# Five-wide u/gate pairs, block sums by accumulating DMAs, and v's scalings behind a bank copy

## The chip, the core and the metric

The kernel runs on one core of one Trainium2 chip. The metric is the device time of one execution in microseconds (us). A core has five engines that take their instructions in order and wait for one another by semaphores: TensorE (PE, the matmuls, with its weight loads shown apart as PEld), VectorE (DVE), ScalarE (ACT), GpSimd (POOL) and SyncE (SP). SP issues the plain loads; POOL issues the DMAs that add into their destination. All transfers are carried by the core's 16 DMA engines.

## The reference

Two layers on 256 tokens of width 2048, all in fp32. Layer 0 is a gated MLP with a causal position mixing, layer 1 a stick-breaking attention. The change lies in layer 0:

```python
proj = rms_norm(x) @ w_in                       # 2048 x 12288: [u | v | gate], 4096 wide each
u, v = gelu(proj[u]), rms_norm(gelu(proj[v]))
mixed = einsum('gts,bnsgc->bntgc', tril(w_s), v in chunks of 128 tokens) + bias   # 16 groups of 256 columns
y = u * mixed * silu(proj[gate])
h = x + y @ w_out
```

The products with `w_in` for u and gate are 2048 x 8192 weights, 64 MB, against 256 tokens.

## The kernel before

**Precision.** An fp32 operand is held as a high part and a rest (hi and lo), both in the fast fp32 format of TensorE, and a product takes three matmuls: hi x hi, lo x hi, hi x lo (`terms`, L119 to L121). The token side is split once. Every weight tile is split as it comes, by `cut` (L108 to L116): ACT casts hi (L114), DVE subtracts to get lo (L115). A cut mostly covers two 128-row tiles, 128 x 1024 elements, and then feeds 12 matmuls in a plain product (two tiles, two blocks of 128 tokens, three terms). There are five hi and five lo buffers.

**Pairs.** The 16 x 512-column blocks of u and gate are worked in eight `Pair`s (L233), numbered from 0; a pair is one block of u (j = 1) and one of gate (j = 0). In a part of a pair's 16 row tiles (k) the four quadrants (upper or lower half of those rows, block 0 or 1) are multiplied by a scheme with seven products in place of eight. `ks` says how many tiles the upper and the lower half each have. The quadrants are called b11, b12 (upper rows, first and second block), b21, b22 (lower rows). The products run in the order p1, p5 (`head`), p6, p2, p7, p3, p4 (`body`), and each takes ks x 3 matmuls. Some of them need sums of quadrants, and these are made in place: b11 becomes a difference of b12 and b11 behind p1 (`minus`, L286), takes b22 in behind p5 (L314), and takes b21 in behind p6 (`minus` again); b12 takes in b22 by an accumulating DMA that reads b22's rows from memory again (`plus`, L294). The tiles of a quadrant are held in groups of two: with ks = 4 there are groups 0 and 1, with ks = 5 a fifth tile is group 2. The fifth of b11 gets b22 by such a DMA as well, since b22's fifth is loaded late.

The row tiles outside the two halves are the "rest", 16 - 2 x ks of them, and are multiplied plainly: `column(0)` behind the body, and `column(1)`, whose steps of two tiles are spread by `run` between the blocks of the next pair. In all a pair has 192 - 3 x ks matmuls.

**Banks.** The products are gathered in banks a, b, c, d, e of the result memory. ACT copies one bank into the next as the scheme wants it (L326 b from a, L331 c from b, L338 d from c, and L328 `es`, a copy of e), and DVE adds es to b and c.

**Mixing.** Behind p4 each pair calls `mixing` (L592): the position weights ws come by a POOL DMA (L597) issued behind the pair's last accumulating one, are masked on POOL (L602), and are split on ACT (wh, L604) and DVE (wl, L605), both held behind the copy to d. v, scaled to its norm, is split into vh (ACT, L610) and vl (DVE, L611). Six matmuls follow (L617 to L619), whose results ACT writes over v (L621). The finished columns go through an activation on ACT (L626) and products on DVE (L628, L533).

**Order.** Every engine's order is fixed when the kernel is built, by a scheduler that simulates the instructions with a model of their durations; `tc.issue_after(x)` holds an instruction behind x on its engine's list. SP's loads are issued in the order of the code. On POOL the accumulating DMAs, ws and the mask stand in one queue.

Of the kernel before, what the change touches and what calls it, by code (L numbers as in the profile page):

```python
# [20 lines left out]
KS_GU = (4, 4, 4, 5, 4, 5, 4, 4)  # L21
# [8 lines left out]
def trunk_kernel(ctx: ExitStack, tc: tile.TileContext, x, xt, gcols, wst, a_w_in, a_v_norm_g,  # L30
# [11 lines left out]
    nc = tc.nc  # L42
# [80 lines left out]
    class Left:  # L123
# [3 lines left out]
        def __init__(self, hi, lo):  # L127
            self.hi, self.lo, self.s, self.ks = hi, lo, [], 0
# [29 lines left out]
        def fifth(self, out, name):
# [8 lines left out]
            nc.vector.tensor_sub(sm[:, 0], a21, a22)  # L167
            nc.vector.tensor_sub(sm[:, 1], a11, sm[:, 0])
# [6 lines left out]
        def sums_of(self, y, ks, out, name):  # L175
# [10 lines left out]
            nc.vector.tensor_sub(s24, a11, s13)  # L186
# [3 lines left out]
            nc.vector.tensor_sub(s24, a12, s24)  # L190
# [42 lines left out]
    class Pair:  # L233
# [50 lines left out]
        def minus(self, into, b0, b1, order=None):  # L284
            for g in order or range(len(self.groups)):
                nc.vector.tensor_sub(into[g], b0[g], b1[g])  # L286

        def plus(self, into, i, j, g0=0):

            for g in self.early:  # L290
                if g < g0:
                    continue
                k, n = self.groups[g]
                adds.append(nc.gpsimd.dma_start(into[g], self.src(HALVES[i][k], n, j), accum_op=ALU.add))  # L294

        def head(self):
# [11 lines left out]
            self.minus(self.b11, self.b12, self.b11, self.early)  # L308
# [4 lines left out]
            for g in range(len(self.b22)):  # L313
                nc.vector.tensor_add(self.b11[g], self.b22[g], self.b11[g])  # L314
            self.plus(self.b11, 1, 1, len(self.b22))

        def body(self, between=lambda: None):
# [21 lines left out]
            self.minus(b11, b21, b11)  # L339
# [247 lines left out]
    with ExitStack() as lg:  # L587
# [4 lines left out]
        def mixing(b, pair):  # L592
# [15 lines left out]
            for t in range(NT):  # L608
                vs = v_of(t, b * CB, CB)
                nc.scalar.activation(vh[:, t], vs, AF.Identity, scale=rv[:, t:t + 1])  # L610
# [581 lines left out]
```

## Time and profile before

| | |
|---|---|
| time, median of 3 runs | 1144.05 us (1144.0 to 1144.16) |
| span of the profiled execution | 1142.0 us |
| time outside the span, against the median | 2.05 us |
| u/gate stage, from the first mixing's end of the windows view to the last | 150.5 to 488.5 us |
| loads by SP's queue (q1) | 227.57 MB, 58.9% of 16 DMA engines |
| by POOL's queue (q0) | 33.04 MB, 16.2% |

The profiled execution's own time is its span; what the device time has beyond it is not in the trace. The views used below are: the page (busy time of each engine; the chain of waits that ended last), the windows view (busy time of each engine in stretches of time, here from one mixing to the next), groups of instructions by line and shape (count, then total busy us, mean ns, and idle time ahead with what ended it), the timeline (start, duration, engine, line, operation; in brackets the idle time ahead and what ended it) and the DMA view (shares, queues, median us from issue to landing). "DVE gu_p_lo" is the lo half of a tile of one of the seven products, "gu_lo" that of a column's tile, "gu_b" a quadrant's tiles.

### The profile page before, as it was taken

How to read it: one execution, taken by the hardware profiler on the slowest of the kernel's cores; microseconds unless marked ns; L12 is line 12 of the kernel's file. 1: busy time of each engine (PE TensorE's matmuls, PEld its weight loads, DVE VectorE, ACT ScalarE, POOL GpSimd, SP SyncE). 2: the span in 40 equal slices, each digit the busy share in tenths (PEclk: the TensorE clock that was granted, in tenths of full speed). 3: DMA queues.
4: the chain of work that ended last, by engine and by line, in shares of the span. 5: the costliest groups of instructions: out<-in, count | busy, mean ns of one | idle time of the engine just before them, and what ended most of it. 6: DMA issues, size and time to landing. Idle time of an engine off the chain costs nothing.

```text
span 1142.0 us, 14838 instructions
## 1 busy us (share of the span) xinstructions
PE 1132.3 (99%) x5168; PEld 937.6 (82%) x5168; DVE 1010.9 (89%) x1111; ACT 828.5 (73%) x1102; POOL 99.8 (9%) x106
## 2 busy tenths in 40 slices
PE   9999999999999999999999999999999999999997
PEld 6788888888888888888888888888888888888886
DVE  7899889988998999978988678989889989897996
ACT  8776777777777778866657456788678887886564
POOL 0100110110110210100010001110100101100000
PEclk9999999999999999999999999999999999999999
DMA  9988788787797797685885868687687776837972
GB/s 335 317 290 270 214 252 270 194 266 241 173 274 249 191 261 240 177 296 142 267 259 166 276 203 282 153 280 211 181 283 200 211 230 174 272 88 241 325 225 92
DMA packets 135659, 264.72 MB, mean 232 GB/s; under 512 B 8992, under 2 KB 9504, under 8 KB 135456
## 3 DMA queue, kind: packets, MB, share of 16 engines
q1 hardware_dynamic: 117472, 227.57, 58.9%
q0 software_dynamic: 16304, 33.04, 16.2%
q10 hardware_dynamic: 1808, 3.17, 0.8%
q8 instruction: 40, 0.66, 0.2%
q14 instruction: 35, 0.29, 0.1%
HBM read 259.55 MB, written 4.19 MB: 231 GB/s over the span
## 4 chain that ended last, share of the span: by engine, by line
PE 93%; DMA 2%; DVE 2%; issue 1%; ACT 1%; SPq 0%; POOLq 0%; POOL 0%; ACTq 0%; DVEq 0%
PE gu_a L119 3%; PE gu_b L119 3%; PE gu_b L121 3%; PE gu_a L121 3%; PE gu_a L120 3%; PE gu_b L120 3%; PE op_acc L119 2%; PE op_acc L120 2%; PE op_acc L121 2%; PE gu_d L119 2%; PE gu_d L121 2%; PE gu_c L121 2%; PE gu_d L120 2%; PE gu_c L119 2%; PE gu_c L120 2%; PE qk_a L121 1%
## 5 line engine op out<-in xcount | busy, mean ns | idle before, releaser
L114 ACT CAST gu_p_hi<-gu_b 128x1024 fp32r<-128x1024 f32 (+1 forms) x126 | 122.9, 1004 | 38.4 <-DVE gu_b L314 16.1
L115 DVE TENSOR_TENSOR gu_p_lo<-gu_b,gu_p_hi 128x1024 fp32r<-128x1024 f32 (+1 forms) x126 | 142.8, 1165 | 1.9 <-ACT gu_p_hi L114 1.2
L115 DVE TENSOR_TENSOR qk_p_lo<-qk_b,qk_p_hi 128x1024 fp32r<-128x1024 f32 (+1 forms) x77 | 80.8, 1073 | 8.9 <-ACT qk_p_hi L114 8.4
L114 ACT CAST qk_p_hi<-qk_b 128x1024 fp32r<-128x1024 f32 (+1 forms) x77 | 70.5, 934 | 19.0 <-DMA qk_b<-in_b_w_in 4.0
L115 DVE TENSOR_TENSOR gu_lo<-gu_raw,gu_hi 128x1024 fp32r<-128x1024 f32 x60 | 72.1, 1218 | 12.5 <-ACT gu_hi L114 12.2
L114 ACT CAST gu_hi<-gu_raw 128x1024 fp32r<-128x1024 f32 x60 | 62.0, 1052 | 21.0 <-DMA gu_raw<-in_a_w_in 11.5
L115 DVE TENSOR_TENSOR v_lo<-v_raw,v_hi 128x1024 fp32r<-128x1024 f32 (+1 forms) x41 | 48.9, 1193 | 15.2 <-ACT v_hi L114 15.2
L114 ACT CAST v_hi<-v_raw 128x1024 fp32r<-128x1024 f32 (+1 forms) x41 | 41.7, 1028 | 27.9 <-DMA v_raw<-in_a_w_in 26.4
L115 DVE TENSOR_TENSOR v_p_lo<-v_b,v_p_hi 128x1024 fp32r<-128x1024 f32 x42 | 50.3, 1220 | 3.3 <-ACT v_p_hi L114 3.1
L114 ACT CAST v_p_hi<-v_b 128x1024 fp32r<-128x1024 f32 x42 | 43.0, 1049 | 9.8 <-PE v_c L121 4.9
L115 DVE TENSOR_TENSOR bg_p_lo<-bg_b,bg_p_hi 128x1024 fp32r<-128x1024 f32 (+1 forms) x42 | 42.5, 1041 | 4.8 <-ACT bg_p_hi L114 4.7
L114 ACT CAST o_p_hi<-o_b 128x1024 fp32r<-128x1024 f32 (+1 forms) x35 | 33.4, 965 | 18.1 <-PE op_acc L121 13.0
L115 DVE TENSOR_TENSOR bv_p_lo<-bv_b,bv_p_hi 128x1024 fp32r<-128x1024 f32 (+1 forms) x42 | 42.5, 1040 | 3.8 <-ACT bv_p_hi L114 3.6
L114 ACT CAST bv_p_hi<-bv_b 128x1024 fp32r<-128x1024 f32 (+1 forms) x42 | 37.4, 908 | 10.0 <-DMA bv_b<-in_b_w_in 3.0
L294 POOL DMA_DIRECT2D gu_b<-in_a_w_in x20 | 23.0, 1155 | 240.2 <-DVE gu_b L286 134.3
L114 ACT CAST bg_p_hi<-bg_b 128x1024 fp32r<-128x1024 f32 (+1 forms) x42 | 37.3, 907 | 8.0 <-PE bg_a L121 2.5
L115 DVE TENSOR_TENSOR o_p_lo<-o_b,o_p_hi 128x1024 fp32r<-128x1024 f32 (+1 forms) x35 | 38.3, 1113 | 5.4 <-ACT o_p_hi L114 5.4
L286 DVE TENSOR_TENSOR gu_b<-gu_b,gu_b 128x1024 f32<-128x1024 f32 (+1 forms) x36 | 41.4, 1169 | 0.1
L114 ACT CAST o_hi<-o_raw 128x1024 fp32r<-128x1024 f32 x22 | 23.0, 1052 | 24.9 <-DMA o_raw<-in_a_w_out 24.8
L115 DVE TENSOR_TENSOR o_lo<-o_raw,o_hi 128x1024 fp32r<-128x1024 f32 x22 | 26.7, 1221 | 15.2 <-ACT o_hi L114 15.0
L114 ACT CAST op_hi<-op_raw 128x1024 fp32r<-128x1024 f32 x24 | 25.1, 1053 | 19.3 <-PE op_acc L121 8.8
L120 PE MATMUL op_acc<-op_lo,yc 128*128 128x512 f32 x96 | 37.8, 393 | 0.0
(798 smaller groups left out, 3797.8 us busy)
## 6 DMA issues: line engine op xcount, KB each, us to landing
gu_b<-in_a_w_in SPq DMA_DIRECT2D x64, 512.0 KB, 4.8
gu_raw<-in_a_w_in SPq DMA_DIRECT2D x60, 512.0 KB, 5.4
v_raw<-in_a_w_in SPq DMA_DIRECT2D x39, 512.0 KB, 5.5
qk_b<-in_b_w_in SPq DMA_DIRECT2D x32, 512.0 KB, 5.3
qk_raw<-in_b_w_in SPq DMA_DIRECT2D x26, 512.0 KB, 5.5
v_b<-in_a_w_in SPq DMA_DIRECT2D x24, 512.0 KB, 5.4
op_raw<-in_a_w_out SPq DMA_DIRECT2D x24, 512.0 KB, 4.9
o_raw<-in_a_w_out SPq DMA_DIRECT2D x22, 512.0 KB, 4.7
```

The costliest lines, as they stand in the source:

```text
L114: nc.scalar.copy(hi[:, sl], raw[:, sl])
L115: low[0] = nc.vector.tensor_sub(lo[:, sl], raw[:, sl], f(hi[:, sl]))
L119: nc.tensor.matmul(acc, lh, hi, start=first, stop=False, skip_group_check=True)
L120: nc.tensor.matmul(acc, lh, lo, start=False, stop=False, skip_group_check=True)
L121: nc.tensor.matmul(acc, ll, hi, start=False, stop=last, skip_group_check=True)
L286: nc.vector.tensor_sub(into[g], b0[g], b1[g])
L294: adds.append(nc.gpsimd.dma_start(into[g], self.src(HALVES[i][k], n, j), accum_op=ALU.add))
```

## The change

There are three edits, all in layer 0's u/gate stage.

1. `KS_GU`, the ks of the eight pairs, goes from (4, 4, 4, 5, 4, 5, 4, 4) to (4, 5, 5, 5, 5, 5, 5, 4). Pairs 1, 2, 4 and 6 get a fifth tile in each half and one column step less in each column.
2. The sum b11 with b21 behind p6 is made by accumulating DMAs (`plus`) for the groups below `FAR_GU[b]`, and by DVE for the others. `FAR_GU` is (0, 2, 2, 1, 2, 1, 2, 1), so 11 groups of 1024 columns go to the POOL queue. [...]
3. vh's scalings are held behind the copy to d, as wh is, and vl follows them.

```diff
-KS_GU = (4, 4, 4, 5, 4, 5, 4, 4)
+KS_GU = (4, 5, 5, 5, 5, 5, 5, 4)
+FAR_GU = (0, 2, 2, 1, 2, 1, 2, 1)
...
-        def plus(self, into, i, j, g0=0):
+        def plus(self, into, i, j, g0=0, g1=9):
 
             for g in self.early:
-                if g < g0:
+                if not g0 <= g < g1:
                     continue
                 k, n = self.groups[g]
                 adds.append(nc.gpsimd.dma_start(into[g], self.src(HALVES[i][k], n, j), accum_op=ALU.add))
...
-            self.minus(self.b11, self.b12, self.b11, self.early)
+            for g in self.early:
+                b = (self.b11[g], self.b12[g])[::1 if g < 2 else -1]
+                nc.vector.tensor_sub(self.b11[g], *b)
             self.plus(self.b12, 1, 1)
...
             for g in range(len(self.b22)):
-                nc.vector.tensor_add(self.b11[g], self.b22[g], self.b11[g])
+                nc.vector.tensor_sub(self.b11[g], self.b11[g], self.b22[g])
             self.plus(self.b11, 1, 1, len(self.b22))
...
-            nc.scalar.copy(es, e)
+            nc.scalar.activation(es, e, AF.Identity, scale=-1.0)
             block(b11, lambda k: left.sum_part(1, k), b, "p6")
+            self.plus(b11, 1, 0, 0, self.far)
...
             self.last_act = nc.scalar.copy(d, c)
-            self.minus(b11, b21, b11)
+            for g in range(self.far, len(self.groups)):
+                (nc.vector.tensor_add if g < 2 else nc.vector.tensor_sub)(b11[g], b21[g], b11[g])
             block(b22, lambda k: left.sum_part(3, k), b, "p3")
...
             for t in range(NT):
                 vs = v_of(t, b * CB, CB)
-                nc.scalar.activation(vh[:, t], vs, AF.Identity, scale=rv[:, t:t + 1])
+                with tc.issue_after(ins_of(pair.last_act)):
+                    nc.scalar.activation(vh[:, t], vs, AF.Identity, scale=rv[:, t:t + 1])
                 nc.vector.scalar_tensor_tensor(vl[:, t], vs, rv[:, t:t + 1], f(vh[:, t]),
                                                op0=ALU.mult, op1=ALU.subtract)
...
-                     lambda j, t, bank, b=b: evac_gu(b, j, t, bank), mid=lambda pair, b=b: mid_gu(b, pair), fifth_first=True))
+                     lambda j, t, bank, b=b: evac_gu(b, j, t, bank), mid=lambda pair, b=b: mid_gu(b, pair), fifth_first=True,
+                     far=FAR_GU[b]))
```

What is left out of the diff are the token side's sums, with their signs turned likewise. Line numbers in the changed kernel are two or three higher from `plus` on to `mixing`, and `plus` itself has L292.

Where the instructions stand. On POOL, the accumulating DMAs of pair 2 (names gu_b_0, gu_b_1 and gu_b_2 are the groups), the position weights and their mask, before:

```order
L294 DMA gu_b_0_2209<-in_a_w_in 128x2x512
L294 DMA gu_b_1_2211<-in_a_w_in 128x2x512
L597 DMA ws_2459<-in_wst 128x256
L602 AFFINE_SELECT ws_2459<-ws_2459 128x256
L294 DMA gu_b_2_2566<-in_a_w_in 128x512
```

and now:

```order
L292 DMA gu_b_2_2254<-in_a_w_in 128x512
L292 DMA gu_b_0_2256<-in_a_w_in 128x2x512
L292 DMA gu_b_1_2258<-in_a_w_in 128x2x512
L292 DMA gu_b_2_2248<-in_a_w_in 128x512
L292 DMA gu_b_0_2250<-in_a_w_in 128x2x512
L292 DMA gu_b_1_2252<-in_a_w_in 128x2x512
L599 DMA ws_2545<-in_wst 128x256
L604 AFFINE_SELECT ws_2545<-ws_2545 128x256
L292 DMA gu_b_2_2634<-in_a_w_in 128x512
```

The pair has gained two DMAs for the fifths (into b12 and b11) and two for the sums behind p6, and ws stands behind them all.

On DVE, the part about p6 of a pair with ks = 5 (pair 3 before; gu_p_lo is a product's cut, gu_112 and gu_114 are tiles of the older pair's column), before:

```order
L115 TENSOR_TENSOR gu_p_lo<-gu_b_0_2562,gu_p_hi 128x1024
L115 TENSOR_TENSOR gu_112_lo<-gu_112_raw,gu_112_hi 128x1024
L286 TENSOR_TENSOR gu_b_0_2562<-gu_b_0_2674,gu_b_0_2562 128x1024
L115 TENSOR_TENSOR gu_p_lo<-gu_b_1_2564,gu_p_hi 128x1024
L115 TENSOR_TENSOR gu_p_lo<-gu_b_2_2560,gu_p_hi 128x512
L115 TENSOR_TENSOR gu_114_lo<-gu_114_raw,gu_114_hi 128x1024
L286 TENSOR_TENSOR gu_b_1_2564<-gu_b_1_2676,gu_b_1_2564 128x1024
L286 TENSOR_TENSOR gu_b_2_2560<-gu_b_2_2755,gu_b_2_2560 128x512
L115 TENSOR_TENSOR gu_p_lo<-gu_b_0_2674,gu_p_hi 128x1024
```

and now, in pair 5, where one group is left to the DMAs:

```order
L116 TENSOR_TENSOR gu_p_lo<-gu_b_0_3390,gu_p_hi 128x1024
L116 TENSOR_TENSOR gu_p_lo<-gu_b_1_3392,gu_p_hi 128x1024
L116 TENSOR_TENSOR gu_p_lo<-gu_b_2_3388,gu_p_hi 128x512
L341 TENSOR_TENSOR gu_b_1_3392<-gu_b_1_3504,gu_b_1_3392 128x1024
L341 TENSOR_TENSOR gu_b_2_3388<-gu_b_2_3566,gu_b_2_3388 128x512
L116 TENSOR_TENSOR gu_114_lo<-gu_114_raw,gu_114_hi 128x1024
L116 TENSOR_TENSOR gu_p_lo<-gu_b_0_3502,gu_p_hi 128x1024
```

Group 0's sum is gone from the list; the sums of groups 1 and 2 still stand ahead of p2's first cut (the last row).

On ACT, the part about p4 and the mixing of pair 4 (wh and vh as above; gu_p_hi is p4's cut of b11's groups, gu_08 to gu_014 are tiles of column 0), before:

```order
L114 CAST gu_p_hi<-gu_b_0_2958 128x1024
L114 CAST gu_p_hi<-gu_b_1_2960 128x1024
L338 COPY gu_d<-gu_c 128x512
L604 CAST wh_3196<-ws_3194 128x256
L114 CAST gu_08_hi<-gu_08_raw 128x1024
L114 CAST gu_010_hi<-gu_010_raw 128x1024
L114 CAST gu_012_hi<-gu_012_raw 128x1024
L621 ACTIVATE v_114<-mix_0_3207,cols 128x2x256
L621 ACTIVATE v_114<-mix_1_3212,cols 128x2x256
L610 ACTIVATE vh_3617<-v_114,nv_r 128x512 x2
L114 CAST gu_014_hi<-gu_014_raw 128x1024
```

and now:

```order
L115 CAST gu_p_hi<-gu_b_0_3010 128x1024
L339 COPY gu_d<-gu_c 128x512
L115 CAST gu_p_hi<-gu_b_1_3012 128x1024
L606 CAST wh_3307<-ws_3305 128x256
L613 ACTIVATE vh_3312<-v_114,nv_r 128x512 x2
L115 CAST gu_p_hi<-gu_b_2_3008 128x512
L115 CAST gu_010_hi<-gu_010_raw 128x1024
L115 CAST gu_012_hi<-gu_012_raw 128x1024
L115 CAST gu_014_hi<-gu_014_raw 128x1024
L624 ACTIVATE v_114<-mix_0_3318,cols 128x2x256
L624 ACTIVATE v_114<-mix_1_3323,cols 128x2x256
```

The two scalings that stood here before belong to the next pair (5) and ran some 40 us ahead of its mixing; now each pair's own stand between wh and p4's last cut.

More of the change, by code (lines that the diff above doesn't have):

```diff
@@ L149, in sums @@
                 nc.vector.tensor_sub(s3, a21, a11)
-                nc.vector.tensor_sub(s2, a11, s1)
-                nc.vector.tensor_sub(s4, a12, s2)
+                nc.vector.tensor_sub(s2, s1, a11)
+                nc.vector.tensor_add(s4, a12, s2)
                 for i, si in enumerate((s1, s2, s3, s4)):
@@ L166, in fifth @@
             a11, a12, a21, a22 = full[:, 0, 0:P], full[:, 1, 0:P], full[:, 0, P:S], full[:, 1, P:S]
-            nc.vector.tensor_sub(sm[:, 0], a21, a22)
-            nc.vector.tensor_sub(sm[:, 1], a11, sm[:, 0])
+            nc.vector.tensor_sub(sm[:, 0], a22, a21)
+            nc.vector.tensor_add(sm[:, 1], a11, sm[:, 0])
             nc.vector.tensor_sub(sm[:, 2], a21, a11)
@@ L185, in sums_of @@
             nc.vector.tensor_sub(s13, a21, a22)
-            nc.vector.tensor_sub(s24, a11, s13)
+            nc.vector.tensor_sub(s24, s13, a11)
             split(0, s13)
@@ L189, in sums_of @@
             nc.vector.tensor_sub(s13, a21, a11)
-            nc.vector.tensor_sub(s24, a12, s24)
+            nc.vector.tensor_add(s24, a12, s24)
             split(2, s13)
@@ L233, in trunk_kernel, with __init__ @@
     class Pair:
-        def __init__(self, src, left, nk, name, ks, evac, mid=None, fifth=None, fifth_first=False):
+        def __init__(self, src, left, nk, name, ks, evac, mid=None, fifth=None, fifth_first=False,
+                     far=0):
             self.fifth = fifth or (lambda j, name: ex.tile([P, 1, CB], F32, tag=f"b1{j + 1}_2", name=name))
             self.src, self.left, self.name, self.ks = src, left, name, ks
-            self.evac, self.mid = evac, mid
+            self.evac, self.mid, self.far = evac, mid, far
             self.rest = [k for k in range(nk) if k not in HALVES[0][:ks] + HALVES[1][:ks]]
@@ L282, in block @@
                 yield
-        def minus(self, into, b0, b1, order=None):
-            for g in order or range(len(self.groups)):
-                nc.vector.tensor_sub(into[g], b0[g], b1[g])
-        def plus(self, into, i, j, g0=0):
+        def plus(self, into, i, j, g0=0, g1=9):
             for g in self.early:
-                if g < g0:
+                if not g0 <= g < g1:
                     continue
```

## The prediction

> **What bounds the kernel now.** I read the page's first two parts, then the chain of waits, then the u/gate stage alone, which is where the change acts.
>
> ```profile
> span 1142.0 us, 14838 instructions
> PE 1132.3 (99%) x5168; PEld 937.6 (82%) x5168; DVE 1010.9 (89%) x1111; ACT 828.5 (73%) x1102; POOL 99.8 (9%) x106
> PE 93%; DMA 2%; DVE 2%; issue 1%; ACT 1%; SPq 0%; POOLq 0%; POOL 0%; ACTq 0%; DVEq 0%
> ```
>
> TensorE (PE) is busy for 99% of the span and carries 93% of the chain. VectorE (DVE) comes next with 89%, so it has some 130 us to spare over the whole, but that says nothing of one pair. The windows view, cut from one pair's mixing to the next, does:
>
> ```profile
> core 0: us, PE busy (x) PEld busy (x) DVE busy (x) ACT busy (x) POOL busy (x), PEclk, DMA share, GB/s
> 194.75:236.91 42.16, 42.16 (x187) 34.91 (x187) 40.95 (x42) 32.07 (x37) 4.22 (x4) 1.00 0.79 236
> 236.91:279.07 42.16, 42.16 (x187) 34.91 (x187) 37.84 (x37) 31.69 (x37) 3.41 (x4) 1.00 0.76 227
> 279.07:325.31 46.24, 46.24 (x205) 38.29 (x205) 42.09 (x45) 34.47 (x43) 5.59 (x6) 1.00 0.80 227
> 362.71:408.95 46.24, 46.24 (x205) 38.29 (x205) 42.36 (x46) 34.35 (x43) 5.83 (x6) 1.00 0.83 239
> sum 338.04, PE 338.04 PEld 279.85 DVE 315.06 ACT 256.83 POOL 39.38; mean PE 42.26 PEld 34.98 DVE 39.38 ACT 32.10 POOL 4.92
> ```
>
> PE's busy time equals the window in every row, at a granted clock of 1.00: over 338 us nothing stalls it, and its matmuls alone set the time. A window runs from one mixing to the next, through the older pair's columns and the new pair's blocks; pairs count from 0. The last row is a 5-wide pair behind a 4-wide. One matmul's price is the distance of two starts, not the 0.39 us that the row shows for its own, since they overlap:
>
> ```profile
> 235.84 0.39 PE L119 MATMUL gu_d<-gu_p_hi,x_hi 128*128 128x512 f32 x1
> 236.07 0.39 PE L120 MATMUL gu_d<-gu_p_lo,x_hi 128*128 128x512 f32 x1
> ```
>
> That is 0.23 us, and the window gives the third digit: 42.16 / 186 = 0.2267, with 186 the matmuls of a 4-wide pair (180) and its mixing (6). The last row holds 46.24 / 0.2267 = 204. A 5-wide behind a 5-wide will have 177 + 6 = 183, or 41.5 us: two column steps of 12 less, one in each column, and three matmuls of p4 more.
>
> **The gain.** A pair has 192 - 3 x ks matmuls. Four pairs go from ks = 4 to 5: 4 x 3 = 12 matmuls fewer, 12 x 0.2267 = 2.72 us, if nothing new stalls. The profiled execution's span is 1142.0 us; the median of the runs shown, 1144.05, lies 2.05 us above, which I carry over. So 1142.0 - 2.72 + 2.05 = 1141.33. What a measurement of this kernel can tell from no change is about 0.2%, 2.29 us: the change counts as faster only if it adds less than 0.43 us of stalls, and as slower only if it adds more than 5.0 us.
>
> **What the change does to the other engines.** Prices, from the groups of the stage (150 to 490 us), with forms kept apart:
>
> ```profile
> L115 DVE TENSOR_TENSOR gu_p_lo<-gu_b,gu_p_hi 128x1024 fp32r<-128x1024 f32 x112 | 134.1, 1221 | 1.9 <-ACT gu_p_hi L114 1.2
> L115 DVE TENSOR_TENSOR gu_p_lo<-gu_b,gu_p_hi 128x512 fp32r<-128x512 f32 x14 | 10.0, 714 | 0.0
> L114 ACT CAST gu_p_hi<-gu_b 128x1024 fp32r<-128x1024 f32 x112 | 115.2, 1052 | 33.8 <-DVE gu_b L314 16.1 <-PE gu_c L121 12.9 <-issue 2.4
> L114 ACT CAST gu_p_hi<-gu_b 128x512 fp32r<-128x512 f32 x14 | 8.7, 621 | 4.6 <-DMA gu_b<-in_a_w_in 3.6 <-PE gu_b L121 1.1
> L286 DVE TENSOR_TENSOR gu_b<-gu_b,gu_b 128x1024 f32<-128x1024 f32 x32 | 38.9, 1229 | 0.1
> L610 ACT ACTIVATE vh<-v,nv_r 128x512 fp32r<-128x512 f32 x16 | 10.7, 719 | 0.0
> L611 DVE SCALAR_TENSOR_TENSOR vl<-v,nv_r,vh 128x512 fp32r<-128x512 f32 x16 | 11.3, 745 | 8.9 <-ACT vh L610 8.9
> L294 POOL DMA_DIRECT2D gu_b<-in_a_w_in x20 | 23.0, 1155 | 240.2 <-DVE gu_b L286 134.3 <-DMA gu_raw<-in_a_w_in 54.2 <-ACT v L481 34.7
> ```
>
> *VectorE in all.* Each widened pair cuts seven 512-wide fifths in place of two 1024-wide column tiles, and sums its fifth twice: 7 x 0.714 - 2 x 1.221 + 2 x 0.7 = 4.0 us, four times 15.8. The 11 sums handed to DMAs are 1024 wide: 11 x 1.229 = 13.5 us back. So +2 us of DVE, while PE needs 2.7 us less. *Per pair* it is tighter. The last window is the model, 42.36 us of DVE with no sum handed away. Behind a 5-wide neighbour two column cuts fall out and a fifth's comes in: 42.36 - 2.44 + 0.71 = 40.6 of PE's 41.5 us. With one sum gone it is 39.4, with two 38.2, so DVE would be 92 to 95% busy, where it reaches 97% now (40.95 of 42.16) with no stall. ScalarE (ACT) has 34.35 - 2 x 1.05 + 0.62 = 32.9 us to do. Both hide behind PE in the mean; what hides them locally is the lead of a cut over its use.
>
> *The lead of the cuts.* The closest places are p7 and p3 of a 5-wide pair. Here the lo half's own row, then the matmul that reads it:
>
> ```profile
> 397.58 1.23 DVE L115 TENSOR_TENSOR gu_p_lo<-gu_b,gu_p_hi 128x1024 fp32r<-128x1024 f32 x1
> 399.72 0.39 PE L120 MATMUL gu_c<-gu_p_lo,xs 128*128 128x512 f32 x1
> 399.32 1.22 DVE L115 TENSOR_TENSOR gu_p_lo<-gu_b,gu_p_hi 128x1024 fp32r<-128x1024 f32 x1
> 401.53 0.39 PE L120 MATMUL gu_b<-gu_p_lo,xs 128*128 128x512 f32 x1
> ```
>
> The first ends at 398.81, 0.91 us ahead; the second at 400.54, 0.99 ahead. Of the two column steps that a 5-wide pair loses behind a 5-wide, the first lies ahead of the older pair's last column tile, where ACT waits for data (409.55, below) and the lead is set anew. The second, in the column run between the new pair's blocks, counts: PE arrives 2.72 us earlier, DVE 1.22 earlier for the cut it saves, and 1.23 (one sum handed over) or 2.46 (two) for the sums, which stand just before p2. The lead becomes 0.91 - 2.72 + 1.22 + 1.23 = 0.64 us, or 1.87. Bounds: if none of the sums' relief reaches this place, -0.6; if the lead also builds over the pair's spare time, 2 and more. I take 0.6 to 1.9, so no stall: the sums stand directly ahead of it in DVE's order.
>
> *v's scalings.* The two vh (ACT) and two vl (DVE) now stand behind the bank copy to d, beside wh, instead of some 40 us ahead of their use:
>
> ```profile
> 401.05 1.06 ACT L114 CAST gu_p_hi<-gu_b 128x1024 fp32r<-128x1024 f32 x1 [0.58 <-PE gu_c L121]
> 402.01 0.59 ACT L338 COPY gu_d<-gu_c 128x512 f32<-128x512 f32 x1
> 402.52 1.05 ACT L114 CAST gu_p_hi<-gu_b 128x1024 fp32r<-128x1024 f32 x1
> 403.47 0.41 ACT L604 CAST wh<-ws 128x256 fp32r<-128x256 f32 x1
> 409.55 1.05 ACT L114 CAST gu_hi<-gu_raw 128x1024 fp32r<-128x1024 f32 x1 [3.25 <-DMA gu_raw<-in_a_w_in]
> 405.06 0.42 DVE L605 TENSOR_TENSOR wl<-ws,wh 128x256 fp32r<-128x256 f32 x1
> 406.29 0.39 PE L617 MATMUL mix<-vh,wh 128*128 128x512 f32 x1
> 415.13 0.39 PE L120 MATMUL gu_a<-gu_lo,x_hi 128*128 128x512 f32 x1
> ```
>
> After wh two vh end at 403.88 + 2 x 0.72 = 405.3, 1.0 us before the mixing reads them. After wl two vl end at 405.48 + 2 x 0.745 = 407.0; PE's new order puts their first use nine matmuls behind the first mixing one, 406.29 + 2.04 = 408.3: 1.3 us of lead. What is queued behind them, p4's last cut and the first column cuts, moves 1.4 us later on both engines; ACT next stands still for 3.25 us at 409.55, so the delay dies there. I take 0; from where the lead is used up, each 0.1 us costs 0.8 us over the eight pairs. A gain there is none, since the work is the same.
>
> *The DMAs.* For the last window above, the DMA view: busy share and GB/s in 40 slices of 1.16 us, queues with packets, MB and share, issues with the us to landing; then rows of the timeline:
>
> ```profile
> DMA  9999926816868999999965003838999999899999
> GB/s 383 392 397 400 363 101 85 315 66 64 158 55 145 207 229 259 198 209 241 271 160 195 0 0 57 278 119 133 383 365 328 358 310 370 161 344 383 376 346 363
> q1 hardware_dynamic: 4856, 9.30, 60.5%
> q0 software_dynamic: 880, 1.70, 21.7%
> gu_b<-in_a_w_in POOLq DMA_DIRECT2D x2, 512.0 KB, 7.9
> ws<-in_wst POOLq DMA_DIRECT2D x1, 128.0 KB, 8.6
> 378.53 0.89 POOL L597 DMA_DIRECT2D ws<-in_wst  x1
> 386.80 1.22 DVE L115 TENSOR_TENSOR gu_p_lo<-gu_b,gu_p_hi 128x1024 fp32r<-128x1024 f32 x1
> 387.23 1.05 POOL L602 TENSOR_SCALAR_AFFINE_SELECT ws<-ws 128x256 f32<-128x256 f32 x1 [7.80 <-DMA ws<-in_wst]
> ```
>
> Plain loads (q1) cost 0.605 x 46.24 / 9.30 = 3.0 us of all 16 DMA engines per MB, accumulating ones (q0) 0.217 x 46.24 / 1.70 = 5.9. A pair's own loads are 8.39 MB whatever its width, 25.2 us; its adds 1.70 MB, 10.0 us. Each far add brings 0.524 MB, 3.1 us. With two, 41.4 us of DMA time in a window of 41.5; with one, 38.3. The other bound: the first slices move 392 GB/s at a share of 9, 2.55 us per MB, which gives 37.6 and 34.5. I take the middle, 0.95 and 0.88 of the window, nearer to what the windows show now (0.83): late loads eat into the leads, but the pair with one add behind each with two gives time to recover.
>
> On this the Trainium skill is milder: "DMA: Bandwidth & Descriptors", Specifications, gives a core about 358 GB/s from HBM. By that page a pair with two far adds would need only 11.14 MB / 41.5 us = 268 GB/s, three quarters of it, and rival B below would have no ground; the accumulating row (170 GB/s) speaks for the dearer reading.
>
> The far adds land in time themselves: the one for p6's second tile may go once that tile is cut, 388.02 by DVE's row; issued within 1 us, it lands 7.9 us later, about 397, and p4's first cast starts at 401.05. ws is issued behind them, at about 390 instead of 378.53, and lands at 398.6 by its 8.6 us; the mask (1.05) has it ready at 399.7, 3.8 us before wh's cast.
>
> The same skill has a rule against moving sums to this queue: "SBUF — State Buffer", in the box on the "DVE blocks DMA" trap, says that GpSimd cannot write a DMA's descriptors while VectorE holds their shared port in a two-port mode. Here L294's issues took 1.155 us in the mean beside a VectorE busy 93% of the stage; by that row the 11 adds cost POOL 13 us out of 338, and by the rule's worst reading they would come later, as in rival D.
>
> **The rivals.** *B: the DMA engines fill.* In pairs 2, 4 and 6 (two far adds) the 41.4 us figure is the true one, the idle slices (the 0s and 3s above) vanish, and the last column tile, for which ACT waits 3.25 us already, comes about 4 us later than now. Its cast and lo cut are done at 410.60 + 1.22 = 411.8 and PE reads it at 415.13, a lead of 3.3, so some 0.7 us stalls there, and up to 0.3 more in the next pair's first loads: 0.5 to 1 us in each of three pairs, 1.5 to 3 us, 1142.8 to 1144.3, say 1143.3. For it speaks the wait at 409.55; against it the slices 21 to 28 (65003838), which still have room. *C: VectorE's lead runs out.* If none of the relief reaches p7 and p3, each of the five 5-after-5 pairs stalls up to the 0.6 us by which that lead falls short: 3.0 us, 1144.3. Against it, the fuller pair 1 runs DVE at 97% now and PE has no gap. *D, the slower one: ws behind the far adds.* If the GpSimd queue moves one transfer after the other, two far adds at 3.1 us each take twice that while SP's loads share the engines, 12.4 us, so that ws lands not at 398.6 but at 390 + 12.4 + 4 = 406.4, the mask and wh end at 407.9, and PE stands 1.6 us at the mixing. The next group's adds wait behind the mask on GpSimd's own order, so p5's and p7's tiles could be late too. 1.6 us in the four pairs with two (1, 2, 4, 6) is 6.4 us; twice over in three of them, 11.2; the middle gives 1141.3 + 8.8 = 1150.1. The point from which it decides: ws landing later than 404.8 (406.29 - 1.05 - 0.41), 15 us after its issue against 8.6 now. Against it: two adds of 512 KB stand in the queue close ahead of ws now, and 8.6 holds them. *That it doesn't do what it says* can be left out: the program has 12 matmuls fewer.
>
> **How the numbers follow.** A, 12 matmuls and no stall above 0.43 us: 0.57, 1141.3, its own range 1140.9 to 1141.8. B 0.20 and C 0.10, both mostly within 0.2%. D 0.13. So faster 0.57; the same 0.29 (B and C but for a hundredth); slower 0.14. The predicted time is A's. The range runs from 1140.9 to 1144.8, which holds A, B and C and leaves D out.
>
> **What would show it.** Right: windows from mixing to mixing of 41.5 us or so for pairs behind a 5-wide one, PE busy equal to the window in each, and 11 sums of 1024 columns missing from VectorE. DMA shares of 0.9 to 0.97 in pairs with two far adds. Waits of ACT for gu_raw longer than 3.2 us point to B; of DVE or PE around p7 and p3 with DMAs in time, to C; of the mask for ws beyond 12 us, or of ACT for the mask, to D. A total above 1141.8 makes the forecast wrong, and PE's gaps in this stage tell by whose hand.

## The result

The changed kernel took 1147.34 us (median; 1145.18 to 1148.36) beside 1144.11 for the kernel before (1143.67 to 1145.79). The ratio on record, which is worked out apart from these medians and from fast executions alone, is 1.0019 with a 95% interval of 1.0010 to 1.0028; the medians would give 1.0028. So it is slower by 0.2 to 0.3%, where 0.24% faster was forecast, and lies above the range. The profiled execution has a span of 1146.2 us, 4.2 more than before. The program does hold 12 matmuls fewer, 2.72 us, so in this execution 6.9 us of new loss have to be found (4.9 us, if one goes by the ratio).

Page of the changed kernel, busy times and chain of waits:

```profile
span 1146.2 us, 14944 instructions
PE 1133.0 (99%) x5156; PEld 933.6 (81%) x5156; DVE 1010.8 (88%) x1128; ACT 832.8 (73%) x1122; POOL 130.9 (11%) x125
PE 67%; DVE 12%; DMA 8%; issue 6%; ACT 4%; POOL 1%; SPq 0%; POOLq 0%; ACTq 0%; DVEq 0%
```

PE still shows 99%, and says nothing: a matmul that waits for its operand counts as busy for part of that time. The chain says more. PE held 93% of it before and holds 67% now, and VectorE, the DMAs and ScalarE stand in it instead. VectorE's total is unchanged (1010.9 before), as the sum of the prediction had it within 2 us. The turned signs in the diff, which go with the DMAs' `ALU.add`, add no work to it.

The windows view over one fixed stretch, 241 to 454 us, which lies in pairs 1 to 6 in every kernel, counts the loss. The count in brackets behind PE's busy time is of matmuls; one that lies across a border counts on both sides, in every kernel alike. Changed kernel:

```profile
241.00:284.00 43.00, 42.72 (x186) 34.17 (x185) 39.20 (x44) 32.90 (x42) 8.03 (x8) 1.00 0.91 258
284.00:326.00 42.00, 41.70 (x184) 34.03 (x183) 39.49 (x43) 33.18 (x43) 6.97 (x7) 1.00 0.89 256
326.00:368.00 42.00, 42.00 (x187) 34.76 (x186) 39.61 (x44) 32.98 (x42) 7.73 (x8) 1.00 0.92 263
368.00:411.00 43.00, 42.32 (x184) 33.95 (x183) 39.10 (x44) 33.03 (x42) 6.83 (x7) 1.00 0.87 246
411.00:454.00 43.00, 42.57 (x186) 34.27 (x185) 38.98 (x43) 32.92 (x42) 7.77 (x8) 1.00 0.92 261
```

These are 927 matmuls. The best version below, which waits nowhere here, does 949 in the same 213 us, and the kernel before 947. 22 missing ones at 0.2267 us are 5.0 us: most of the 6.9. (The distances from one start to the next, added up over the stretch, exceed 0.2267 us each by 4.9 us in all, and by nothing in the kernel before.) The others lie outside the stretch. The largest single one seen stands at the start of the next stage (waits of PE, 490 to 600 us: total, times, longest):

```profile
PE yT L436 <- DVE yc L577: 0.9, 1, 0.9
```

What PE's weight loads waited for in that stretch of the changed kernel (total, times, longest; the three largest of five rows):

```profile
PEld gu_b L121 <- DVE gu_lo L116: 3.0, 4, 0.9
PEld gu_c L121 <- DVE gu_p_lo L116: 1.4, 4, 0.5
PEld gu_b L120 <- ACT gu_p_hi L115: 1.0, 3, 0.3
```

No transfer stands here: it is VectorE's lo halves that come late, most of all those of column tiles (gu_lo), then those of p7 (gu_c <- gu_p_lo). ScalarE's hi halves have the rest, 1.8 us. In the timeline of pair 5 two such places, VectorE's row and then PE's (the column tiles still belong to pair 4):

```profile
379.13 1.22 DVE L116 TENSOR_TENSOR gu_lo<-gu_raw,gu_hi 128x1024 fp32r<-128x1024 f32 x1
380.40 0.50 PE L121 MATMUL gu_b<-gu_lo,x_hi 128*128 128x512 f32 x1 [0.23 <-DVE gu_lo L116]
392.60 1.22 DVE L116 TENSOR_TENSOR gu_lo<-gu_raw,gu_hi 128x1024 fp32r<-128x1024 f32 x1
393.87 0.50 PE L121 MATMUL gu_b<-gu_lo,x_hi 128*128 128x512 f32 x1 [0.45 <-DVE gu_lo L116]
```

PE starts 0.05 us after the lo half is done: the lead is gone. VectorE is busy 39.0 to 39.6 us in these windows of 42 and 43, so it should have had time; the question is when it lost it. Walking back along its row from 380 there is no gap until the seam between the pairs (p4 and the last columns of pair 4, then p1 of pair 5). Timeline of the changed kernel there:

```profile
365.27 0.67 DVE L116 TENSOR_TENSOR gu_p_lo<-gu_b,gu_p_hi 128x512 fp32r<-128x512 f32 x1
361.98 4.33 SPq L224 DMA_DIRECT2D gu_b<-in_a_w_in  x4
365.98 0.34 SPq L224 DMA_DIRECT2D gu_b<-in_a_w_in  x1
368.61 1.05 ACT L115 CAST gu_hi<-gu_raw 128x1024 fp32r<-128x1024 f32 x1 [2.77 <-DMA gu_raw<-in_a_w_in]
372.60 0.62 ACT L115 CAST gu_p_hi<-gu_b 128x512 fp32r<-128x512 f32 x1 [1.78 <-DMA gu_b<-in_a_w_in]
373.25 0.69 DVE L116 TENSOR_TENSOR gu_p_lo<-gu_b,gu_p_hi 128x512 fp32r<-128x512 f32 x1 [2.33 <-ACT gu_p_hi L115]
```

The second row holds four loads, of which the last, shown by itself in the third row, is that of pair 5's fifth tile of b11. It is issued the moment the first row ends, p4's last cut in pair 4, which reads that pair's fifth: the tile has one buffer. In the code this load stands first among the pair's loads, but on SP's list it has become the last of these four: its buffer comes free only with p4's last cut. It lands 6.6 us after its issue, 4.1 us behind the load of the last column tile, and since p1 takes the fifth first, ACT waits 1.78 us and VectorE 2.33. VectorE's waits of this kind in the fixed stretch, five of the seven at the five seams (2.1 to 2.3 us each):

```profile
DVE gu_p_lo L116 <- ACT gu_p_hi L115: 12.5, 7, 2.3
```

The same place in the kernel before:

```profile
361.31 0.48 SPq L223 DMA_DIRECT2D gu_b<-in_a_w_in  x1
366.67 1.05 ACT L114 CAST gu_hi<-gu_raw 128x1024 fp32r<-128x1024 f32 x1 [1.21 <-DMA gu_raw<-in_a_w_in]
367.62 0.62 ACT L114 CAST gu_p_hi<-gu_b 128x512 fp32r<-128x512 f32 x1
```

There pair 4 is four wide, so the buffer had long been free, the load went out 5.4 us ahead of the last column tile's cast (now 2.6), landed 0.7 us behind that tile, and p1's cast followed without a wait.

### The profile page after: what moved, and what is told of

The parts are those of the page before. It is cut to its first block, busy times and chain, and to the rows that moved or that the text cites. A ratio compares the mean times of both kernels' runs of the same rounds, so it can differ in the third digit from the quotient of the medians.

```text
span 1146.2 us, 14944 instructions
## 1 busy us (share of the span) xinstructions
PE 1133.0 (99%) x5156; PEld 933.6 (81%) x5156; DVE 1010.8 (88%) x1128; ACT 832.8 (73%) x1122; POOL 130.9 (11%) x125
## 4 chain that ended last, share of the span: by engine, by line
PE 67%; DVE 12%; DMA 8%; issue 6%; ACT 4%; POOL 1%; SPq 0%; POOLq 0%; ACTq 0%; DVEq 0%
DVE gu_p_lo L116 6%; DMA gu_b<-in_a_w_in 5%; DMA gu_raw<-in_a_w_in 2%; ACT gu_p_hi L115 2%; PE op_acc L122 2%; PE op_acc L120 2%; PE op_acc L121 2%; DVE gu_lo L116 1%; PE qk_a L122 1%; PE qk_a L121 1%; PE qk_b L121 1%; PE qk_b L122 1%; PE qk_b L120 1%; PE qk_a L120 1%; PE f_acc L120 1%
## 5 line engine op out<-in xcount | busy, mean ns | idle before, releaser
L116 DVE TENSOR_TENSOR gu_p_lo<-gu_b,gu_p_hi 128x1024 fp32r<-128x1024 f32 x154 | 160.3, 1077 | 15.0 <-ACT gu_p_hi L115 14.2
L115 ACT CAST gu_p_hi<-gu_b 128x1024 fp32r<-128x1024 f32 x154 | 136.5, 934 | 50.4 <-DVE gu_b L314 32.2
L116 DVE TENSOR_TENSOR gu_lo<-gu_raw,gu_hi 128x1024 fp32r<-128x1024 f32 x52 | 62.6, 1217 | 12.7 <-ACT gu_hi L115 12.2
L115 ACT CAST gu_hi<-gu_raw 128x1024 fp32r<-128x1024 f32 x52 | 53.6, 1050 | 24.8 <-DMA gu_raw<-in_a_w_in 18.6
L292 POOL DMA_DIRECT2D gu_b<-in_a_w_in x39 | 43.2, 1122 | 229.5 <-ACT gu_p_hi L115 92.4
L292 POOL DMA_DIRECT2D qk_b<-in_b_w_in x14 | 15.0, 1097 | 206.1 <-DVE qk_b L308 113.1
```

Source lines behind the costliest of these rows:

```text
L115: nc.scalar.copy(hi[:, sl], raw[:, sl])
L116: low[0] = nc.vector.tensor_sub(lo[:, sl], raw[:, sl], f(hi[:, sl]))
```

## The experiments

Three theories went into the first runs. S, the seam: the fifth's one buffer costs the starting lead. V: VectorE has too much to do in a 41.5 us pair. D: the DMA engines are full. In the diffs below the changed kernel is the base unless another is named. Each ratio is to the kernel before, run beside it; that kernel's median was 1144.7 to 1145.1 there, up to 1 us above the 1144.1 from which the expectations start.

**A second buffer for the fifth.**

```diff
-            self.fifth = fifth or (lambda j, name: ex.tile([P, 1, CB], F32, tag=f"b1{j + 1}_2", name=name))
+            self.fifth = fifth or (lambda j, name: ex.tile([P, 1, CB], F32, tag=f"b1{j + 1}_2", bufs=2 - j if far else 1, name=name))
...
-            wl = pb.tile([P, GPB, P], F32R, tag="wl", name=f"wl{b}")
+            wl = pb.tile([P, GPB, P], F32R, tag="wl", bufs=1, name=f"wl{b}")
```

> The changed kernel with a second buffer for the fifth tile of b11 (and one buffer instead of two for wl, which makes room). Theory S (the seam): in the trace of the changed kernel the load of that fifth is issued at 365.98, the moment p4's last lo cut of the pair ahead frees its only buffer (DVE 365.27 + 0.67), lands at 372.6, and ACT and with it DVE stand about 2 us for it at each seam between two 5-wide pairs; this lead is missing later, at the column tiles and at p7. It expects some 2 us of lead back in five pairs, most of the 5 us of stalls gone, 1142 to 1143.5 us. Theory V (VectorE's work as such is too much for a 41.5 us pair): the work is the same, 1146.5 to 1148. Theory D (the DMA engines are full, share 0.91): another load will be late in its place, 1146 to 1148.

1142.28 us, ratio to the kernel before 0.9979 (0.9970 to 0.9989), as S expected and neither V nor D did. The seam between pairs 4 and 5 in its timeline:

```profile
358.05 0.46 SPq L224 DMA_DIRECT2D gu_b<-in_a_w_in  x1
364.60 1.05 ACT L115 CAST gu_hi<-gu_raw 128x1024 fp32r<-128x1024 f32 x1 [1.75 <-PE mix L622]
365.56 0.61 ACT L115 CAST gu_p_hi<-gu_b 128x512 fp32r<-128x512 f32 x1
366.83 0.68 DVE L116 TENSOR_TENSOR gu_p_lo<-gu_b,gu_p_hi 128x512 fp32r<-128x512 f32 x1
```

The fifth's load goes out ahead of the pair's other first loads, right behind that of the last column tile, and neither engine waits for it. In the fixed stretch there are 943 matmuls. The six that are still missing (1.4 us) are lost at the last column tile of pair 5, at p7 of pairs 5 and 6, and most of all at p1 of pair 7, which waits 0.7 us for ScalarE's hi half.

**v's scalings early again**, that is, without the third edit:

```diff
-                with tc.issue_after(ins_of(pair.last_act)):
-                    nc.scalar.activation(vh[:, t], vs, AF.Identity, scale=rv[:, t:t + 1])
+                nc.scalar.activation(vh[:, t], vs, AF.Identity, scale=rv[:, t:t + 1])
```

> The changed kernel without its third edit: vh is not held behind the bank copy, so vh and vl run early again, out of p4. S: vl's 1.4 us no longer stand ahead of p4's last cut on VectorE, so the fifth's load is issued some 1.4 us sooner and each of five pairs gets that lead: 1143.5 to 1145.5. V: the same VectorE work in a pair, only elsewhere: 1147. D: 1147.

1151.77 us, ratio 1.0059 (1.0040 to 1.0078): 4 us worse than the changed kernel, where S had promised a gain. All three theories missed it, and it is taken up again below.

**All sums back on VectorE**, `FAR_GU = (0, 0, 0, 0, 0, 0, 0, 0)`.

> The changed kernel with all 11 sums back on VectorE. V: 1.2 to 2.5 us more VectorE work in each of seven pairs, of which little is covered: 1152 to 1158. S: the seam is as it was, and the lead it lacks is needed more: 1150 to 1156. D: the DMA share of the pairs falls from 0.91 to about 0.84 and the loads come in time: 1143 to 1145.

1156.9 us, ratio 1.0102 (1.0086 to 1.0117). D is out by 12 us. The 11 sums are 13.5 us of VectorE's time and cost 9.5 us of the kernel's: with the seam as it is, some seven tenths of what is added to VectorE in these pairs comes out as time.

**Without b22's adds into b12.**

```diff
-            self.plus(self.b12, 1, 1)
+            if not self.far:
+                self.plus(self.b12, 1, 1)
```

> The changed kernel, leaving out the accumulating DMAs that add b22 into b12 in the pairs with far sums (five tiles in a 5-wide pair, 1.3 MB; their products then work on b12 alone). Matmuls and VectorE's work are unchanged. D: about 7.7 us of DMA time less per pair, so the late loads are in time and the stalls go: 1142 to 1143.5. S: the fifth's load still starts only when its buffer is free, its landing is faster by a microsecond at most: 1145.5 to 1147. V: 1147.

1146.39 us, ratio 1.0008 (0.9996 to 1.0020). The DMA share, 0.87 to 0.92 in the stretch before, is 0.71 to 0.75; the fourth part of the windows view of this run,

```profile
368.00:411.00 43.00, 42.37 (x185) 34.15 (x184) 39.44 (x43) 33.36 (x43) 4.06 (x4) 1.00 0.72 226
```

shows it. The time is 1 us lower, as S expected (D: 1142 to 1143.5), and the intervals do not tell that from no difference. The wait at the seam stays, as the timeline shows for pair 5's fifth:

```profile
371.35 2.52 ACT L115 CAST gu_p_hi<-gu_b 128x512 fp32r<-128x512 f32 x3 [1.79 <-DMA gu_b<-in_a_w_in]
```

What the run does not do is to lighten the engines at the seam itself. From 357 to 374 us the plain loads alone fill them (6.60 of 6.62 MB; the busy share is at 9 in all 40 slices):

```profile
DMA packets 3438, 6.62 MB, mean 390 GB/s; under 512 B 214, under 2 KB 214, under 8 KB 3436
```

There the fifth lands 6.5 us after its issue, 0.7 us behind the load ahead of it, while the median of the 256 KB loads over this pair is 4.3 us. With that landing it would have been in before ScalarE stood still (an estimate from these rows). So the queue ahead of the fifth seems to be a part of the wait, and no run here tests it by itself.

**The changed kernel once more**, run beside the next three.

> The changed kernel itself once more, as the measure for the others on this chip: 3 us (0.2 to 0.3%) over the kernel before, as first measured.

1147.35 us, ratio 1.0017 (1.0006 to 1.0028).

**Two buffers, and two far sums in all 5-wide pairs**: the second-buffer kernel with `FAR_GU = (0, 2, 2, 2, 2, 2, 2, 1)`.

> Two buffers for b11's fifth, and two far sums in every 5-wide pair (2 and 1 before). With the second buffer alone, the leads start at 4 to 6 us in pair 5 and are used up at the last column tile and p7 (0.06), with 1.2 us of stalls left in pairs 5 and 6, and none in pairs 1 to 4. Joint theory (the seam takes the starting lead, VectorE's work then wears it down): 1.2 us less VectorE work in pairs 3 and 5 ends these stalls, 1141.0 to 1141.7 where the kernel before has 1144.1. Seam alone: as with two buffers alone, some 1.2 us more. D: one more far sum in two pairs brings late loads, 1142 to 1144.

1141.78 us, ratio 0.9970 (0.9958 to 0.9981): the fastest version, and faster than both kernels. The number lies between what the joint theory gave (up to 1141.7) and D (from 1142), so the windows have to decide. The profiled execution, the fastest of six, has a span of 1138.9 us, within 0.4 of the 1139.3 that the prediction reached for a kernel without stalls; the median of the six spans is 1140.1. Its windows of the fixed stretch, three of five:

```profile
span 1138.9 us, 14943 instructions
...
241.00:284.00 43.00, 43.00 (x192) 35.59 (x191) 41.00 (x45) 35.95 (x46) 7.56 (x8) 1.00 0.97 279
...
368.00:411.00 43.00, 43.00 (x191) 35.59 (x191) 39.68 (x44) 34.62 (x43) 8.62 (x8) 1.00 0.95 270
411.00:454.00 43.00, 43.00 (x192) 35.59 (x191) 40.27 (x43) 34.00 (x42) 8.03 (x8) 1.00 0.93 260
```

PE is busy in the whole of every window (187 matmuls in each of the two left out), at DMA shares of 0.93 to 0.97, which are higher than those of the changed kernel. So the lead was worn down by VectorE's sums from the level at which the seam left it: S and V together. D, full engines as a cause by themselves, is out; as the reason why a load that goes out late also lands late they stay in.

**Narrow products.** All four of a pair's products with the activated gate and u columns (two for each) are done on 64 of 512 columns; the rest of the output is left without them.

```diff
-                nc.vector.tensor_mul(y, y, sg)
+                nc.vector.tensor_mul(y[:, 0:64], y[:, 0:64], sg[:, 0:64])
...
-                queue.append((1, lambda: times(y, sg)))
+                queue.append((1, lambda: times(y[:, 0:64], sg[:, 0:64])))
```

> The changed kernel with VectorE's four products per pair of the finished u and gate columns done on 64 of 512 columns only (the rest of the output is left unscaled), some 2.2 us less VectorE work per pair; buffers and loads as in the changed kernel. Two of the four stand ahead of p5, two ahead of p7. Joint theory: about 1.1 us of lead comes back ahead of p5 and as much ahead of p7, so most stalls at the column tiles 112 and 114 and at p71 go, that at 110 stays: 1143.5 to 1145. Seam alone, with VectorE's load of no account: as the changed kernel, 1146.5 to 1148.

1143.24 us, ratio 0.9976 (0.9964 to 0.9988), 0.3 us under the joint theory's range; 941 matmuls in the stretch. Some 2.2 us less VectorE work a pair heals about as much as 2 us more lead at the seam (ratio 0.9979, 943 matmuls). One can be paid with the other.

**The old widths**, `KS_GU = (4, 4, 4, 5, 4, 5, 4, 4)`, with the second and third edits kept.

> The changed kernel with the old widths (4, 4, 4, 5, 4, 5, 4, 4), that is, the second and third edits alone: no two 5-wide pairs stand behind each other, so no fifth waits for its buffer, and the number of matmuls is the old one. Seam and joint theory: no stalls, as the kernel before, 1144.1 within 0.5. D: the far adds and POOL's queue cost by themselves, 1145 to 1147.

1145.52 us, ratio 1.0008 (0.9998 to 1.0017), with 948 matmuls in the stretch. The bare number lies in D's range and not in that of S; beside the kernel before (1145.06 here) it cannot be told from no change, and PE waits nowhere in the stretch. So the far sums, POOL's queue and the moved scalings show no cost of their own; where no two 5-wide pairs stand behind each other, there is no stall.

**Two buffers without far sums.**

> Two buffers for b11's fifth and all 11 far sums back on VectorE: the widths and the buffer alone. Joint theory: the starting lead of 2 us more a pair is used up by the 1.2 to 2.5 us of sums that come back, and VectorE has 40.6 of 41.5 us to do: stalls of 1 to 2 us a pair, 1147 to 1152, clearly under the 1156.9 with one buffer. Seam alone: 1142 to 1143.

1152.36 us, ratio 1.0053 (1.0030 to 1.0077), just above the top of what the joint theory gave. The second buffer is worth 4.5 us here as well (1156.9 without it), and the far sums 10 us on top of it.

**Fifth last.** One buffer, `fifth_first=False`: p1 and p5 take the fifth tile behind the two others.

> The changed kernel, one buffer, but p1 and p5 take the fifth tile last and not first; its load stands behind the pair's other first loads in SP's order as before. Joint theory: PE needs the fifth 1.8 us (8 matmuls) to 2.7 us (12) later, and ACT can cast the two others of p1 meanwhile, so about 2 us of the seam's wait are hidden: 1142.5 to 1145. If the wait is not what takes the lead: 1146.5 to 1148.

1144.3 us, ratio 0.9990 (0.9973 to 1.0007); 942 matmuls. The fifth lands 5.4 us after its issue, ahead of its cast. A change of order without any memory hides most of the wait, as expected, but leaves no gain that can be told from none. (The order of the pair's first sums and adds moves with it.)

**Seven pairs of five.** Two buffers, two far sums, and pair 7 five wide.

> Two buffers, two far sums everywhere, and pair 7 five wide as well: 3 matmuls fewer, 0.68 us, than with two buffers and two far sums, if the last pair has the lead: 1141.0 to 1141.8 beside 1144.1 to 1145 for the kernel before. If the last pair, whose mixing the next stage follows, runs out of lead: 1142 to 1144.

1143.96 us, ratio 0.9988 (0.9978 to 0.9999). The u/gate stage has no stall in the stretch (947 matmuls, as in the kernel before), but the loss comes back behind it: in this run PE's waits between 490 and 600 us are

```profile
PE op_acc L120 <- ACT yc L576: 1.5, 1, 1.5
PE yT L436 <- DVE yc L577: 0.5, 1, 0.5
```

where the version with six 5-wide pairs shows none. That is the second of the two outcomes written down, at its place behind the last pair.

**The scalings, taken apart.** First, two buffers with v's scalings early:

> Two buffers for b11's fifth, without the third edit (vh and vl early again, at the seam between two pairs). The run without the third edit and one buffer took 1151.8, for the scalings stand at the seam, where ACT and VectorE wait for the fifth and lead is missing. Joint theory: with the second buffer the seam has 2 us of lead to spend, so most of that loss goes: 1142 to 1145. If the third edit's worth has nothing to do with the seam, the loss of 4 to 5 us stays: 1146 to 1148.

1147.98 us, ratio 1.0032 (1.0020 to 1.0044), 5.7 us over its partner. The second buffer does not pay for it, so the joint theory's reading of the third edit fell. VectorE's row at the seam of this run shows why:

```profile
370.95 1.23 DVE L116 TENSOR_TENSOR gu_lo<-gu_raw,gu_hi 128x1024 fp32r<-128x1024 f32 x1 [2.88 <-ACT gu_hi L115]
...
373.93 0.69 DVE L308 TENSOR_TENSOR gu_b<-gu_b,gu_b 128x512 f32<-128x512 f32 x1 [1.15 <-DMA gu_b<-in_a_w_in]
374.54 1.41 DVE L613 SCALAR_TENSOR_TENSOR vl<-v,nv_r,vh 128x512 fp32r<-128x512 f32 x2
```

VectorE now idles 2.88 us for the last column tile and 1.15 for a quadrant's tile, and *then* does vl's 1.41 us. Taken out of p4, the work leaves a hole ahead of a wait for data; put behind that wait, it eats lead. VectorE's waits for a column tile's hi half between 241 and 454 us, over five seams:

```profile
DVE gu_lo L116 <- ACT gu_hi L115: 11.2, 5, 2.9
```

Two more runs tell VectorE's half from ScalarE's. One makes vl on 64 columns only and lets its matmuls read vh:

```diff
-                nc.vector.scalar_tensor_tensor(vl[:, t], vs, rv[:, t:t + 1], f(vh[:, t]),
+                nc.vector.scalar_tensor_tensor(vl[:, t, 0:64], vs[:, 0:64], rv[:, t:t + 1], f(vh[:, t, 0:64]),
...
-                nc.tensor.matmul(mp, wh[:, j, :], vl[:, :, sl], start=False, stop=False)
+                nc.tensor.matmul(mp, wh[:, j, :], vh[:, :, sl], start=False, stop=False)
```

> Two buffers and v's scalings early (1148.0), but with vl made on 64 of 512 columns and its matmuls reading vh in its place, so VectorE's 1.4 us at the seam shrinks to some 0.3; ACT's vh stays at the seam. If the loss of 5.7 us against the scalings behind the bank copy is VectorE's work between the wait for the last column tile and the tight head: most of it goes, 1142 to 1144. If it is ACT's 1.33 us of vh, ahead of p1's and p5's casts: 1147 to 1148.5.

1143.55 us, ratio 0.9986 (0.9971 to 1.0002). The other leaves vh early and holds vl alone behind the addition of es to c:

```diff
-            nc.vector.tensor_add(c, c, es)
+            self.last_c = nc.vector.tensor_add(c, c, es)
...
-                nc.vector.scalar_tensor_tensor(vl[:, t], vs, rv[:, t:t + 1], f(vh[:, t]),
-                                               op0=ALU.mult, op1=ALU.subtract)
+                with tc.issue_after(ins_of(pair.last_c)):
+                    nc.vector.scalar_tensor_tensor(vl[:, t], vs, rv[:, t:t + 1], f(vh[:, t]),
+                                                   op0=ALU.mult, op1=ALU.subtract)
```

> Two buffers; vh early on ACT at the seam, but vl held on VectorE behind the addition of es to c in p4, where the third edit has it too. VectorE reading: 1142 to 1144, as the second half of the third edit is kept. ACT reading: 1147 to 1148.5. If either half is worth its own 0.4 to 0.7 us a pair: between, 1144 to 1146.

1143.51 us, ratio 0.9989 (0.9974 to 1.0003). The same wait of VectorE in this run:

```profile
DVE gu_lo L116 <- ACT gu_hi L115: 4.0, 4, 1.8
```

vl fills the hole again. In the run with the narrow vl that wait is as long as with the full one,

```profile
DVE gu_lo L116 <- ACT gu_hi L115: 12.5, 6, 3.2
```

and yet the time is good: the idle time ahead of the data is harmless, the work behind it is not. Both runs say VectorE: of the 5.7 us, about 4.4 (5 by the ratios) are vl's place on it. The remaining 1 us or so may be vh's place on ScalarE, but these intervals do not settle it. Why the last column tile itself lands when it does, so that every kernel waits for it somewhere, was not tried.

## Why the prediction was wrong

**The gain was right, and so was the bound.** 12 matmuls are worth 2.72 us; with the fifth's second buffer and the last VectorE stalls gone, the time falls by 0.30% (0.19 to 0.42), where 0.24% was forecast. That the profiled span of 1138.9 comes so near to the forecast's 1139.3 is in part luck, since it is the fastest of six.

**The step that failed** is in the part on the lead of the cuts, on the two column steps that fall out: "the first lies ahead of the older pair's last column tile, where ACT waits for data (409.55, below) and the lead is set anew." The lead was taken to be set anew at the level of the row it was read from, 0.91 us at p7. That row belongs to pair 5 of the kernel before, behind a 4-wide one, where the fifth's buffer is free. Behind a 5-wide pair there is one more wait, for the buffer, which the list of waits in the prediction did not hold. VectorE stands still for it 2.1 to 2.3 us at each of five seams, a term that the sum put at nothing. Repairing it alone turned 1147.3 into 1142.3. How much of the wait is the late issue and how much the full queue in which the load then stands stays open.

**The forecast leads.** 0.64 us at p7 of a pair with one far sum, 1.87 with two, "so no stall". In pair 5, with one, PE takes p7's second lo half the moment it is there (timeline of the changed kernel, VectorE's row and PE's):

```profile
399.76 1.21 DVE L116 TENSOR_TENSOR gu_p_lo<-gu_b,gu_p_hi 128x1024 fp32r<-128x1024 f32 x1
401.03 0.50 PE L121 MATMUL gu_c<-gu_p_lo,xs 128*128 128x512 f32 x1
```

The lead is 401.03 - 400.97 = 0.06 us, and the matmul's 0.50 us in place of 0.39 marks the wait.

The places watched, p7 and p3, were not the worst either: the column tiles between the new pair's blocks, at 380.40 and 393.87, lose more, and the prediction gave them no sum.

**The rivals.** C, VectorE's lead, was the right mechanism with a chance of 0.10, at a wrong place and for half a reason: its price of 3.0 us was for relief that doesn't arrive, while the sums' relief did arrive (the run with all sums back on VectorE would not be 9.5 us slower otherwise) and the starting lead did not. B, full DMA engines, had its stalls at the last column tile and up to 0.3 us at the next pair's first loads. As a cause by itself it fell with the two runs on either side: 7.7 us less DMA time a pair gained 1 us at most, and a share of 0.97 stalled nothing. But the loads at the seam do come one behind another on full engines, and the late one among them is the one that p1 takes first: there B was near the place, and its price too small. D fell by its own point, 15 us from the issue of ws to its landing. Timeline of the changed kernel, pair 5:

```profile
389.97 1.10 POOL L599 DMA_DIRECT2D ws<-in_wst  x1
395.54 0.81 POOL L604 TENSOR_SCALAR_AFFINE_SELECT ws<-ws 128x256 f32<-128x256 f32 x1 [4.47 <-DMA ws<-in_wst]
404.90 0.41 ACT L606 CAST wh<-ws 128x256 fp32r<-128x256 f32 x1
```

ws was issued at 389.97 (forecast about 390) and was in 5.5 us later (8.6); its mask was done 8.5 us ahead of wh's cast. Pair 5 has one far sum; in pair 2, with two, ws took 7.1 us.

**DMA prices.** In pair 2 of the changed kernel the DMA view has the two queues at

```profile
q1 hardware_dynamic: 4268, 8.17, 52.2%
q0 software_dynamic: 1424, 2.75, 38.5%
```

of 42.7 us: 2.73 us per MB for plain loads, between the forecast's bounds of 2.55 and 3.0, and 6.0 for accumulating ones against 5.9. The volumes were right (2.75 MB for the adds, 8.17 against 8.39 for the loads). A share near 1 was not yet a stall here.

Of the Trainium skill's figure that the prediction set against this ("DMA: Bandwidth & Descriptors", Specifications, about 358 GB/s to a core), the trace shows single slices of 1.1 us at 406 GB/s in the version with two far sums, so here it is no ceiling. The Trainium skill's "Perfetto Trace Analysis", Roofline, agrees with the measurement: it calls the 358 a share with both cores of a pair at work, which a single core may pass. The Trainium skill's other trap, GpSimd locked out by VectorE ("SBUF — State Buffer", the box on "DVE blocks DMA"), did not show: the stage's accumulating issues took 1.122 us in the mean, beside 1.155 before. No run here shows VectorE in a two-port mode, though, so the trap was not put to the test.

**v's scalings.** The leads were forecast as 1.0 us for vh and 1.3 for vl. Timeline of the changed kernel, pair 5:

```profile
405.20 1.34 ACT L613 ACTIVATE vh<-v,nv_r 128x512 fp32r<-128x512 f32 x2
407.57 1.40 DVE L614 SCALAR_TENSOR_TENSOR vl<-v,nv_r,vh 128x512 fp32r<-128x512 f32 x2
407.95 0.62 PE L620 MATMUL mix<-vh,wh 128*128 128x512 f32 x2
409.99 0.39 PE L621 MATMUL mix<-vl,wh 128*128 128x512 f32 x1
```

vh is 1.4 us ahead of its use and vl 1.0, so the move itself stalls nothing. "I take 0 [...] A gain there is none, since the work is the same" was wrong for these widths: placed behind the seam's wait the same work costs 4 to 6 us more than in p4. It is what kept the changed kernel from being slower still. With the old widths the second and third edits together changed nothing that could be told.

## What to carry to other kernels

When a step is repeated back to back that used to have another between, list the buffers whose next load must wait for the last reader of the step ahead, and read its price (landing time less lead) before any engine's total. A lead read from one neighbour may not be carried over to another. Where the waiting load stands in its queue belongs to that price. And the place of an instruction has a price even where its engine's total does not change: in these runs work ahead of a wait for data was free, and work behind it was taken from the lead.

## What the runs showed of the hardware

Two things are worth keeping. The 16 DMA engines held a mean share of 0.97 and 279 GB/s over 43 us, with slices up to 406 GB/s, nearly a quarter of the bytes (2.75 of 12.02 MB) being accumulating ones, without one stall of TensorE:

```profile
GB/s 406 389 379 383 389 151 103 154 97 204 189 168 234 212 225 189 181 19 40 122 204 194 204 227 354 375 362 383 402 400 394 383 387 389 349 391 385 394 389 381
DMA packets 6254, 12.02 MB, mean 279 GB/s; under 512 B 435, under 2 KB 435, under 8 KB 6250
...
q0 software_dynamic: 1424, 2.75, 37.6%
```

(DMA view of the version with two buffers and two far sums, 241 to 284 us.) And TensorE's busy share is a poor sign of its stalls: the page has 99% both with and without 5 us of waits in this stage, and in the fixed stretch the busy time misses only 1.7 of the 5 us. A matmul's row is 0.39 us long at starts 0.23 apart, so a short wait leaves no gap between rows, and one that waits shows as longer (0.50 us). Counting matmuls in a fixed stretch found them.
